# One level of Strassen's algorithm in the gate and up projections of both feed-forward blocks

## The chip, the core and the metric

The kernel runs on one core of a Trainium2 chip. The metric is the device time of one execution in microseconds (us); three runs of the kernel before gave 1392.4, 1393.01 and 1395.76 us, so its median is 1393.01 us. Everything is float32 at the borders.

## The reference, cut to what matters

One encoder layer over 512 tokens of width 1024. It begins and ends with a SwiGLU feed-forward block of inner width 2816; between them stands the token mixing (three kinds of attention, gates, an output projection), which the change leaves alone.

```python
def swiglu(x, w_gate, w_up, w_down):
    return (jax.nn.silu(x @ w_gate) * (x @ w_up)) @ w_down

h = layer_norm(ALPHA * h + 0.5 * swiglu(h, ffn1_w_gate, ffn1_w_up, ffn1_w_down), ln1_g, ln1_b)
mix = token_mixing(h, mem, ...)
h = layer_norm(ALPHA * h + mix, ln2_g, ln2_b)
h = layer_norm(ALPHA * h + 0.5 * swiglu(h, ffn2_w_gate, ffn2_w_up, ffn2_w_down), ln3_g, ln3_b)
```

## The kernel before

Activations lie transposed: xT is 8 tiles (index k) of 128 features by 512 tokens. Every float32 operand of a matmul is held as a pair: hi, the value rounded to float32r by ACT, and lo, the remainder, taken by DVE. A product of two pairs is three matmuls (mm3, L87 to L92): hi by hi, hi by lo, lo by hi, all into one PSUM bank.

Weights come in chunks of 512 KB. wload (L69) gives one load on SP's queue into raw, a ring of 3 buffers; then ACT writes whi (L79) and DVE writes wlo (L80), rings of 4. PE and SP run in the order in which the program is written; ACT, DVE and POOL are ordered by the scheduler, which wload asks to place its work 200 instructions ahead (AHEAD).

A feed-forward block (class FFN, L163) has 22 column tiles f. For each f, mms (L175) runs 8 k for the gate and 8 for the up projection, 48 matmuls of 512 columns, into two banks. act (L180) takes silu of the gate on ACT (L183), multiplies with the up projection on DVE (L184) and splits the result at once into the pair hh, hl, which is kept for all 22 f. down (L195) then multiplies by w_down, once per half of the output width, in 11 chunks c of two f each, with the token tiles t as banks; half of LN (L124) takes the sums out.

The first block starts with hand-written small loads and conversions (xk, wk, L230 to L249). Then come tiles f = 1 to 21 (L256), LN "a" with its pool and the two loads of gain and bias (L113, L114), and two calls of down. The second block runs f = 0 and 1 in two token halves of 256 columns (L901 to L919, while the last token tiles of the normalisation are still on their way), then f = 2 to 21, LN "c", a whole down and then two partial ones: three token tiles, then the last token tile alone with the normalisation of the other three between its chunks.

Pools are a stack on the left side of SBUF and one on the right; a tile that takes the place of a closed pool's tile waits for that tile's last use (`reuse_waits` "tile", L40).

Of the kernel before, what the change touches and what calls it, by code (L numbers as in the profile page):

```python
# [33 lines left out]
def build(tc, a, out):  # L34
# [18 lines left out]
    edge = pool("edge", side="right").tile([P, 24], F32, name="edge")  # L53
    nc.gpsimd.memset(edge, 0.0)
# [14 lines left out]
    def wload(src, n=D, hp=None, lp=None, eng=None, parts=1):  # L69
        with tc.high_priority(offset=AHEAD):  # L70
            raw = wp.tile([P, D], F32, name="raw", tag="raw", bufs=3)
# [91 lines left out]
    class FFN:  # L163
        def __init__(self, n, stack, xT, wgu, wd):
            self.n, self.xT, self.wgu, self.wd = n, xT, wgu, wd
            self.pl = pool("ffn" + n, stack=stack, side="right")
            self.h = {}

        def weight(self, f, j, parts=1):
            return [x.rearrange("p (k c) -> p k c", c=P) for x in wload(self.wgu[f, j], parts=parts)]  # L170

        def weights(self, f):
            return [self.weight(f, j) for j in range(2)]

        def mms(self, w, ps, c):  # L175
            for j in range(2):
                for k in range(KT):
                    mm3(ps[j][:, c], pick(w[j], A, k), pick(self.xT, A, k, c), k == 0, k == KT - 1)

        def act(self, f, ps):  # L180
            sg = self.pl.tile([P, S], F32, name=f"sg{f}", tag="sg", bufs=2)
            hv = self.pl.tile([P, S], F32, name=f"hv{f}", tag="hv", bufs=2)
            nc.scalar.activation(sg, ps[0], AF.Silu)  # L183
            nc.vector.tensor_tensor(out=hv, in0=ps[1], in1=sg, op=OP.mult)  # L184
            h = (self.pl.tile([P, S], F32R, name=f"hh{f}"), self.pl.tile([P, S], F32R, name=f"hl{f}"))
            split(h[0], h[1], hv)
            self.h[f] = h

        def tiles(self, f0, f1):
            for f in range(f0, f1):  # L190
                ps = [bank(f"gu{f}"), bank(f"gv{f}")]
                self.mms(self.weights(f), ps, A)
                self.act(f, ps)

        def down(self, hf, toks, done, order=range(NF // 2), have={}, dest={}, mid=None):  # L195
            ps = {t: bank(f"dn{t}") for t in toks}
            kept = {}
            for n, c in enumerate(order):
                if mid is not None and n in mid:
                    mid[n]()  # L200
                kept[c] = w = have[c] if c in have else [x.rearrange("p (k c) -> p k c", c=S) for x in wload(self.wd[hf, c], **dest.get(c, {}))]
                for j in range(2):
                    f = 2 * c + j
                    for t in toks:
                        mm3(ps[t], pick(self.h[f], A, slice(t * P, (t + 1) * P)), pick(w, A, j),
                            n == 0 and j == 0, n == NF // 2 - 1 and j == 1)
# [9 lines left out]
    s_x = ExitStack()  # L216
    xp = pool("xraw", stack=s_x)

# [4 lines left out]
    xr = xp.tile([P, KT, S], F32, name="xr")  # L223
    wr = [xp.tile([P, D], F32, name=f"wr{j}") for j in range(2)]
    w0 = [[wp.tile([P, D], F32R, name="whi", tag="whi", bufs=4), wp.tile([P, D], F32R, name="wlo", tag="wlo", bufs=4)] for j in range(2)]
    s_ln = ExitStack()
    s_f = ExitStack()
    f1 = FFN("1", s_f, xT, a["wgu1"], a["wd1"])

# [5 lines left out]
    def wk(j, c):  # L235
        nc.sync.dma_start(wr[j][:, c], a["wgu1"][0, j][:, c])
        conv(w0[j][0][:, c], w0[j][1][:, c], wr[j][:, c])

    wk(0, slice(0, 128))
    xk(0, 1)  # L240
    wk(0, slice(128, 512))
    wk(1, slice(0, 512))
    xk(1, 2)
    xk(2, 4)
    wk(0, slice(512, 1024))
    wk(1, slice(512, 1024))
# [3 lines left out]
    s_x.close()  # L250
    ps = [bank("gu0"), bank("gv0")]
    for k in range(KT):
        for j in range(2):
            mm3(ps[j], [x.rearrange("p (k c) -> p k c", c=P)[:, k] for x in w0[j]], pick(xT, A, k), k == 0, k == KT - 1)
    f1.act(0, ps)
    f1.tiles(1, NF)  # L256
# [646 lines left out]
    s_f = ExitStack()  # L903
    f2 = FFN("2", s_f, h2T, a["wgu2"], a["wd2"])
# [11 lines left out]
    for f in range(NS):  # L916
        f2.mms(ws[f], pss[f], slice(256, 512))
        f2.act(f, pss[f])
    s_l2.close()  # L919
    f2.tiles(NS, NF)  # L920
    s_l3 = ExitStack()
    ln3 = LN("c", s_l3, a["ln3_g"], a["ln3_b"], h2_d, spill=out)
# [21 lines left out]
def _pack(inputs):  # L944
# [16 lines left out]
    for i in (1, 2):  # L961
        g, u, d = (f(f"ffn{i}_w_{n}")[0] for n in ("gate", "up", "down"))
        A[f"wgu{i}"] = np.stack([fm(g), fm(u)], 1)
# [68 lines left out]
```

## Time and profile before

| | us |
|---|---|
| median of 3 runs | 1393.01 |
| the profiled execution, its own time | 1392.8 |
| its span, from first to last instruction | 1391.0 |
| PE busy | 1374.2 |
| DVE busy | 656.3 |
| ACT busy | 476.1 |
| POOL busy | 48.8 |

PE is TensorE's matmuls, PEld its weight loads, DVE VectorE, ACT ScalarE, POOL GpSimd, SP the queue of loads. Matmuls overlap, so what one costs in a dense row is the distance from one start to the next, not its duration. In the views of waits the numbers are us in all, times, longest. In the views of stretches an engine's number is its busy time, with its instructions in brackets, then the granted TensorE clock (1.00 is 2.4 GHz, 0.50 is 1.2 GHz), the busy share of the DMA engines and GB/s.

### The profile page before, as it was taken

The numbers are of one execution on the slowest core, as the hardware profiler recorded it, in microseconds if no ns is written. First come the engines' busy times: TensorE is split into PE (matmuls) and PEld (weight loads), VectorE is DVE, ScalarE is ACT, GpSimd is POOL, SyncE is SP. The second block draws the span as 40 slices with busy tenths as digits, with TensorE's granted clock in tenths as the row PEclk, the third lists the DMA queues.
The fourth block names the chain that finished last, engine by engine and source line by source line (L and its number), as shares of the span: only waits on it lengthen the run. The fifth ranks groups of instructions, "written<-read, shape, count | busy, mean of one in ns | idle before, by whom it ended". The sixth has DMA issues, their size and how long they took to land.

```text
span 1391.0 us, 16204 instructions
## 1 busy us (share of the span) xinstructions
PE 1374.2 (99%) x6488; PEld 1152.0 (83%) x6488; DVE 656.3 (47%) x1055; ACT 476.1 (34%) x734; POOL 48.8 (4%) x70
## 2 busy tenths in 40 slices
PE   8999999999999999999999999999999999999997
PEld 6888888888888878988899878888798888888886
DVE  5333333242567995435454655546763333332325
ACT  5222322221245674324334433333342232222210
POOL 0000000000011001001100000000000000000001
PEclk9999999999999999999999999999999999999999
DMA  6323234333346226332223223223743323333241
GB/s 218 101 91 106 92 94 142 112 128 125 113 171 178 59 60 84 106 96 84 80 76 114 77 83 109 74 84 107 256 168 105 105 93 98 100 121 126 90 163 61
DMA packets 49899, 154.80 MB, mean 111 GB/s; under 512 B 9888, under 2 KB 10528, under 8 KB 49824
## 3 DMA queue, kind: packets, MB, share of 16 engines
q1 hardware_dynamic: 44064, 149.51, 32.8%
q0 software_dynamic: 5760, 4.26, 2.3%
q8 instruction: 51, 0.84, 0.2%
q14 instruction: 24, 0.20, 0.0%
HBM read 143.23 MB, written 7.37 MB: 108 GB/s over the span
## 4 chain that ended last, share of the span: by engine, by line
PE 76%; issue 15%; DMA 4%; DVE 3%; ACT 1%; POOL 1%; POOLq 0%; SPq 0%; DVEq 0%; ACTq 0%
PE dn L91 6%; PE dn L92 6%; PE dn L90 6%; PE gu L90 6%; PE gu L91 5%; PE gu L92 5%; PE gv L92 5%; PE gv L90 5%; PE gv L91 5%; DMA x<-dst 2%; PE g L92 2%; PE g L90 2%; PE g L91 2%; PE y L92 1%; PE y L91 1%
## 5 line engine op out<-in xcount | busy, mean ns | idle before, releaser
L79 ACT ACTIVATE whi<-raw 128x1024 fp32r<-128x1024 f32 x237 | 251.3, 1060 | 693.7 <-issue 199.6
L80 DVE TENSOR_TENSOR wlo<-raw,whi 128x1024 fp32r<-128x1024 f32 x237 | 289.6, 1224 | 406.8 <-ACT whi L79 405.8
L90 PE MATMUL dn<-whi,hh 128*128 128x512 f32 x320 | 126.3, 395 | 0.0
L92 PE MATMUL dn<-whi,hl 128*128 128x512 f32 x320 | 126.3, 395 | 0.0
L91 PE MATMUL dn<-wlo,hh 128*128 128x512 f32 x320 | 126.3, 395 | 0.0
L184 DVE TENSOR_TENSOR hv<-gv,sg 128x512 f32<-128x512 f32 x42 | 29.0, 692 | 139.2 <-PE gv L92 138.5
L90 PE MATMUL g<-uh,whi 128*128 128x512 f32 x192 | 75.3, 392 | 0.0
L90 PE MATMUL dp<-uh,whi 128*128 128x512 f32 x192 | 75.1, 391 | 0.0
L92 PE MATMUL g<-uh,wlo 128*128 128x512 f32 x192 | 74.9, 390 | 0.0
L91 PE MATMUL g<-ul,whi 128*128 128x512 f32 x192 | 74.8, 390 | 0.0
L92 PE MATMUL dp<-uh,wlo 128*128 128x512 f32 x192 | 74.7, 389 | 0.0
L91 PE MATMUL dp<-ul,whi 128*128 128x512 f32 x192 | 74.7, 389 | 0.0
L90 PE MATMUL gu<-xh,whi 128*128 128x512 f32 x176 | 69.3, 394 | 4.5 <-ACT xh L220 4.5
L91 PEld LDWEIGHTS dn<-wlo,hh 128*128 128x128 f32 x320 | 60.3, 188 | 14.2
L90 PEld LDWEIGHTS dn<-whi,hh 128*128 128x128 f32 x320 | 60.3, 188 | 14.1
L92 PEld LDWEIGHTS dn<-whi,hl 128*128 128x128 f32 x320 | 60.3, 188 | 14.0
L90 PE MATMUL gv<-xh,whi 128*128 128x512 f32 x176 | 69.1, 393 | 0.3 <-ACT whi L220 0.3
L91 PE MATMUL gu<-xl,whi 128*128 128x512 f32 x176 | 69.3, 394 | 0.0
L92 PE MATMUL gu<-xh,wlo 128*128 128x512 f32 x176 | 69.0, 392 | 0.0
L91 PE MATMUL gv<-xl,whi 128*128 128x512 f32 x176 | 68.9, 392 | 0.0
L92 PE MATMUL gv<-xh,wlo 128*128 128x512 f32 x176 | 68.9, 392 | 0.0
L90 PE MATMUL gu<-h2h,whi 128*128 128x512 f32 x160 | 62.3, 389 | 0.0
(797 smaller groups left out, 2809.0 us busy)
## 6 DMA issues: line engine op xcount, KB each, us to landing
raw<-in_wgu SPq DMA_DIRECT2D x86, 512.0 KB, 3.5
raw<-in_wd SPq DMA_DIRECT2D x47, 512.0 KB, 3.6
raw<-in_wg SPq DMA_DIRECT2D x24, 512.0 KB, 3.7
raw<-in_wdqk SPq DMA_DIRECT2D x24, 512.0 KB, 3.6
raw<-in_wo SPq DMA_DIRECT2D x16, 512.0 KB, 4.3
raw<-in_wv SPq DMA_DIRECT2D x12, 512.0 KB, 3.5
raw<-in_wbr SPq DMA_DIRECT2D x12, 512.0 KB, 3.4
raw<-in_wmk SPq DMA_DIRECT2D x4, 512.0 KB, 3.4
```

The costliest lines, as they stand in the source:

```text
L79: nc.scalar.activation(hi[:, c], raw[:, c], AF.Copy)
L80: (eng or nc.vector).tensor_tensor(out=lo[:, c], in0=raw[:, c], in1=hi[:, c].bitcast(F32), op=OP.subtract)
L90: nc.tensor.matmul(ps, lh, rh, start=first, stop=False, **kw)
L91: nc.tensor.matmul(ps, lh, rl, start=False, stop=False, **kw)
L92: nc.tensor.matmul(ps, ll, rh, start=False, stop=last, **kw)
L184: nc.vector.tensor_tensor(out=hv, in0=ps[1], in1=sg, op=OP.mult)
```

## The change

The input of a block is cut into four quarters (two token halves of 256 by two halves of k), the weights of one f into four blocks (two halves of k by gate and up). For f = 2 to 21 of the first block and f = 3 to 21 of the second, 39 in all, seven products of 12 matmuls of 256 columns (quads) take the place of the 48 matmuls of 512 columns. The sums of the input's quarters are made once per block (sums). The sums of the weights are made for each f (quad_w): three loads on SP, two accumulating DMAs from POOL, two additions on DVE, and then the splits. In the second block the input is first put together again from its pair. The product h is kept in float32 (ha, hb) and split only in down (h_pair). The raw ring moves to a pool of its own on the right; the weights of one f are stored as two chunks, one for each half of k.

```diff
-            h = (self.pl.tile([P, S], F32R, name=f"hh{f}"), self.pl.tile([P, S], F32R, name=f"hl{f}"))
-            split(h[0], h[1], hv)
-            self.h[f] = h
+            nc.vector.tensor_tensor(out=self.h(f), in0=ps[1], in1=sg, op=OP.mult)
...
+        def open(self, stack):
+            n = self.n
+            self.sr = pool("sumr" + n, stack=stack, side="right")
+            self.q = pool("quad" + n, stack=stack)
+            self.X = {i: tuple((self.q if i in (5, 7) else self.sr).tile([P, 4, 256], F32R, name=f"x{i}{z}{n}") for z in "hl") for i in (5, 7, 3, 6)}
+            self.t4 = tuple(self.q.tile([P, 2, S], F32R, name=f"t4{z}{n}") for z in "hl")
+            self.m = {i: self.q.tile([P, 2, 256], F32, name=f"m{i}{n}") for i in (1, 5, 6)}
+
+        def sums(self, xr):
...
+            nc.vector.tensor_tensor(out=t[5], in0=q[1, 1], in1=q[1, 0], op=OP.subtract)
+            split(*self.X[5], t[5])
+            nc.vector.scalar_tensor_tensor(out=t[6], in0=q[0, 0], scalar=-1.0, in1=t[5], op0=OP.mult, op1=OP.subtract)
+            split(*self.X[6], t[6])
+            nc.vector.scalar_tensor_tensor(out=t[3], in0=t[6], scalar=-1.0, in1=q[0, 1], op0=OP.mult, op1=OP.subtract)
+            split(*self.X[3], t[3])
+            nc.vector.tensor_tensor(out=t[7], in0=q[0, 0], in1=q[1, 0], op=OP.subtract)
+            split(*self.X[7], t[7])
...
+        def quad_w(self, f):
+            src = self.wgu[f]
+            with tc.high_priority(offset=AHEAD):
+                r1 = rawp.tile([P, D], F32, name="raw", tag="raw", bufs=3)
+                r3 = rawp.tile([P, D], F32, name="raw", tag="raw", bufs=3)
+                r2 = self.q.tile([P, D], F32, name="raw2", tag="raw2")
+                r4 = self.q.tile([P, S], F32, name="raw4", tag="raw4")
+                nc.sync.dma_start(r1, src[:, :D])
+                nc.sync.dma_start(r2[:, S:], src[:, 3 * S:])
+                nc.sync.dma_start(r3, src[:, S:3 * S])
+                nc.gpsimd.dma_start(r1[:, S:], src[:, :S], accum_op=OP.add)
+                nc.gpsimd.dma_start(r3[:, :S], src[:, 3 * S:], accum_op=OP.add)
+                nc.vector.tensor_tensor(out=r2[:, :S], in0=r1[:, S:], in1=r2[:, S:], op=OP.add)
...
+                split(*w1, r1)
+                w2 = (self.q.tile([P, D], F32R, name="w2h", tag="w2h", bufs=2), self.q.tile([P, D], F32R, name="w2l", tag="w2l", bufs=2))
+                split(*w2, r2)
+                nc.vector.tensor_tensor(out=r4, in0=r2[:, :S], in1=r3[:, S:], op=OP.add)
...
+                split(*w3, r3)
+                w4 = tuple(x[:, f % 2] for x in self.t4)
+                split(*w4, r4)
...
+        def quads(self, f0, f1):
+            def finish(f, W, a, u, sg):
+                self.prod(a, W, 4)
+                nc.scalar.activation(sg[:, 256:], a, AF.Silu)
+                nc.vector.tensor_tensor(out=self.h(f), in0=u, in1=sg, op=OP.mult)
...
+                self.prod(a, W, 1, True)
+                nc.scalar.activation(m[1], a, AF.Copy)
+                self.prod(c, W, 5, True)
+                nc.scalar.activation(m[5], c, AF.Copy)
+                if prev is not None:
+                    finish(*prev)
+                self.prod(a, W, 6)
+                nc.scalar.activation(m[6], a, AF.Copy)
+                self.prod(c, W, 3)
+                nc.vector.scalar_tensor_tensor(out=u[:, :256], in0=c, scalar=-1.0, in1=m[6], op0=OP.mult, op1=OP.subtract)
+                self.prod(d, W, 2)
+                nc.vector.tensor_tensor(out=sg[:, :256], in0=d, in1=m[1], op=OP.add)
+                nc.scalar.activation(sg[:, :256], sg[:, :256], AF.Silu)
+                self.prod(a, W, 7)
+                nc.vector.scalar_tensor_tensor(out=u[:, 256:], in0=a, scalar=-1.0, in1=m[5], op0=OP.mult, op1=OP.subtract)
+                prev = (f, W, a, u, sg)
+            finish(*prev)
...
+        def h_pair(self, c, lo, hi):
+            t = [self.hc.tile([P, 2, S], F32R, name=f"hc{z}", tag=f"hc{z}", bufs=2) for z in "hl"]
+            src = (self.ha if c < 7 else self.hb)[:, 2 * (c % 7):2 * (c % 7) + 2, lo:hi]
+            split(t[0][:, :, lo:hi], t[1][:, :, lo:hi], src)
...
+                with tc.high_priority(offset=AHEAD // 2):
+                    h = self.h_pair(c, toks[0] * P, (toks[-1] + 1) * P)
...
-    f1.tiles(1, NF)
+    f1.sums(xr)
+    f1.tiles(1, 2)
+    f1.quads(2, NF)
+    s_q.close()
+    f1.open_down(s_ln)
...
+    f2.open(s_q)
...
+            nc.vector.tensor_tensor(out=f2.hb[:, k, s_], in0=h2T[0][:, k, s_].bitcast(F32), in1=h2T[1][:, k, s_].bitcast(F32), op=OP.add)
+    f2.sums(f2.hb)
+    f2.tiles(NS, NS + 1)
+    f2.quads(NS + 1, NF)
+    s_q.close()
     s_l3 = ExitStack()
+    f2.open_down(s_l3)
     ln3 = LN("c", s_l3, a["ln3_g"], a["ln3_b"], h2_d, spill=out)
```

## Rows read from the trace of the kernel before

**Rows 1.** The page, busy time of each engine and its share

```profile
PE 1374.2 (99%) x6488; PEld 1152.0 (83%) x6488; DVE 656.3 (47%) x1055; ACT 476.1 (34%) x734; POOL 48.8 (4%) x70
```

**Rows 2.** The view of waits, PE alone

```profile
PE gu L90 <- ACT xh L220: 4.5, 2, 4.4
```

**Rows 3.** The timeline of DVE in the first block: start us, us, instruction

```profile
107.02 0.69 DVE L184 TENSOR_TENSOR hv<-gv,sg 128x512 f32<-128x512 f32 x1 [3.37 <-PE gv L92]
...
117.91 0.69 DVE L184 TENSOR_TENSOR hv<-gv,sg 128x512 f32<-128x512 f32 x1 [3.37 <-PE gv L92]
```

**Rows 4.** The timeline of PE, matmuls of 256 columns, in two places

```profile
370.91 0.28 PE L90 MATMUL mkps<-memh,whi 128*128 128x256 f32 x1
...
374.44 0.28 PE L90 MATMUL mkps<-memh,whi 128*128 128x256 f32 x1
...
1018.93 0.28 PE L90 MATMUL hu<-h2h,whi 128*128 128x256 f32 x1
...
1021.69 0.28 PE L92 MATMUL hu<-h2h,wlo 128*128 128x256 f32 x1
```

**Rows 5.** The page, costliest groups: the two halves of a weight split

```profile
L79 ACT ACTIVATE whi<-raw 128x1024 fp32r<-128x1024 f32 x237 | 251.3, 1060 | 693.7 <-issue 199.6
L80 DVE TENSOR_TENSOR wlo<-raw,whi 128x1024 fp32r<-128x1024 f32 x237 | 289.6, 1224 | 406.8 <-ACT whi L79 405.8
```

**Rows 6.** Instructions by tile, duration ns (least/median/most): 256 columns out of PSUM

```profile
L284 ACT ACTIVATE mk<-mkps x4: 363/364/364, 374.8 to 383.3; 128x256 f32<-128x256 f32 x4
...
L628 DVE TENSOR_TENSOR dp<-ds,bias x16: 410/415/421, 636.3 to 796.6; 128x256 f32<-128x256 f32 x16
```

**Rows 7.** The view of DMA issues: queue, count, KB each, median us to landing

```profile
raw<-in_wgu SPq DMA_DIRECT2D x86, 512.0 KB, 3.5
...
k<-kr POOLq DMA_DIRECT2D x8, 128.0 KB, 2.4
...
bias<-in_dbias POOLq DMA_DIRECT2D x4, 256.0 KB, 5.3
...
uel<-ul POOLq DMA_DIRECT2D x2, 256.0 KB, 6.7
...
cb<-in_ln_b SPq DMA_DIRECT2D x1, 512.0 KB, 6.2
```

**Rows 8.** The timeline of SP's queue, end of the gate and up part

```profile
212.86 0.43 SPq L67 DMA_DIRECT2D ag<-in_ln_g  x1
...
217.93 22.09 SPq L76 DMA_DIRECT2D raw<-in_wd  x5
...
1207.87 16.64 SPq L76 DMA_DIRECT2D raw<-in_wgu  x4
...
1225.04 0.42 SPq L67 DMA_DIRECT2D cb<-in_ln_b  x1
```

**Rows 9.** The timeline of PE, its first matmuls and its last

```profile
4.37 0.80 PE L90 MATMUL gu<-xh,whi 128*128 128x512 f32 x1 [4.37 <-ACT xh L220]
...
11.06 0.61 PE L92 MATMUL gv<-xh,wlo 128*128 128x512 f32 x1
11.48 0.42 PE L90 MATMUL gu<-xh,whi 128*128 128x512 f32 x1
...
1382.38 0.40 PE L92 MATMUL dn<-whi,hl 128*128 128x512 f32 x1
```

**Rows 10.** Busy time in stretches: PE, PEld, DVE, ACT, POOL, clock, DMA

```profile
0.00:30.00 30.00, 25.14 (x94) 19.00 (x95) 15.30 (x18) 16.31 (x20) 0.37 (x6) 1.00 0.73 243
...
1015.00:1043.00 28.00, 27.09 (x218) 26.31 (x217) 18.01 (x26) 9.71 (x13) 2.77 (x2) 1.00 0.39 137
...
1375.00:1380.00 5.00, 5.00 (x23) 4.07 (x22) 4.67 (x7) 0.00 (x0) 2.16 (x2) 1.00 0.27 111
...
1385.00:1387.00 2.00, 0.00 (x0) 0.00 (x0) 1.56 (x3) 0.00 (x0) 1.26 (x1) 1.00 0.00 0
1387.00:1389.00 2.00, 0.00 (x0) 0.00 (x0) 0.71 (x2) 0.00 (x0) 0.00 (x0) 0.52 0.55 206
```

More of the change, by code (lines that the diff above doesn't have):

```diff
@@ L53, in build @@
     edge = pool("edge", side="right").tile([P, 24], F32, name="edge")
+    rawp = pool("rawp", side="right")
     nc.gpsimd.memset(edge, 0.0)
@@ L70, in wload @@
         with tc.high_priority(offset=AHEAD):
-            raw = wp.tile([P, D], F32, name="raw", tag="raw", bufs=3)
+            raw = rawp.tile([P, D], F32, name="raw", tag="raw", bufs=3)
             hi = wp.tile([P, D], F32R, name="whi", tag="whi", bufs=4) if hp is None else hp
@@ L166, in __init__, with h @@
             self.pl = pool("ffn" + n, stack=stack, side="right")
-            self.h = {}
-        def weight(self, f, j, parts=1):
-            return [x.rearrange("p (k c) -> p k c", c=P) for x in wload(self.wgu[f, j], parts=parts)]
+            self.ha = self.pl.tile([P, 14, S], F32, name=f"ha{n}")
+            self.hb = self.pl.tile([P, 8, S], F32, name=f"hb{n}")
+        def h(self, f):
+            return self.ha[:, f] if f < 14 else self.hb[:, f - 14]
         def weights(self, f):
-            return [self.weight(f, j) for j in range(2)]
+            return [[x.rearrange("p (j k c) -> p j k c", j=2, c=P) for x in wload(self.wgu[f][:, i * D:(i + 1) * D])] for i in range(2)]
         def mms(self, w, ps, c):
@@ new lines, in prod @@
+        def prod(self, ps, W, i, first=False):
+            for k in range(4):
+                mm3(ps, pick(W[i], A, k), pick(self.X[i], A, k), first and k == 0, k == 3, skip_group_check=True)
+        def quads(self, f0, f1):
[3 more added lines that the diff above has]
+                nc.vector.tensor_tensor(out=self.h(f), in0=u, in1=sg, op=OP.mult)
+            prev = None
+            for f in range(f0, f1):
+                W = self.quad_w(f)
+                b1, b2 = bank(f"ga{f}"), bank(f"gc{f}")
+                a, d, c = b1[:, :256], b1[:, 256:], b2[:, :256]
+                m = {i: x[:, f % 2] for i, x in self.m.items()}
+                u = self.q.tile([P, S], F32, name=f"u{f}", tag="u", bufs=2)
+                sg = self.q.tile([P, S], F32, name=f"sg{f}", tag="sg", bufs=2)
+                self.prod(a, W, 1, True)
[15 more added lines that the diff above has]
+            finish(*prev)
@@ L221, in conv @@
         nc.vector.tensor_tensor(out=lo, in0=raw, in1=hi.bitcast(F32), op=OP.subtract)
-    xr = xp.tile([P, KT, S], F32, name="xr")
-    wr = [xp.tile([P, D], F32, name=f"wr{j}") for j in range(2)]
-    w0 = [[wp.tile([P, D], F32R, name="whi", tag="whi", bufs=4), wp.tile([P, D], F32R, name="wlo", tag="wlo", bufs=4)] for j in range(2)]
     s_ln = ExitStack()
     s_f = ExitStack()
+    s_q = ExitStack()
     f1 = FFN("1", s_f, xT, a["wgu1"], a["wd1"])
+    f1.open(s_q)
+    xr = f1.hb
+    wr = [rawp.tile([P, D], F32, name="raw", tag="raw", bufs=3) for j in range(2)]
+    w0 = [[wp.tile([P, D], F32R, name="whi", tag="whi", bufs=4), wp.tile([P, D], F32R, name="wlo", tag="wlo", bufs=4)] for j in range(2)]
     def xk(k0, k1):
@@ L917, in build @@
         f2.mms(ws[f], pss[f], slice(256, 512))
+    s_l2.close()
+    f2.open(s_q)
+    for f in range(NS):
         f2.act(f, pss[f])
-    s_l2.close()
-    f2.tiles(NS, NF)
+    for j in range(2):
+        for c in range(2):
+            k, s_ = slice(4 * j, 4 * j + 4), slice(256 * c, 256 * c + 256)
+            nc.vector.tensor_tensor(out=f2.hb[:, k, s_], in0=h2T[0][:, k, s_].bitcast(F32), in1=h2T[1][:, k, s_].bitcast(F32), op=OP.add)
[3 more added lines that the diff above has]
+    s_q.close()
     s_l3 = ExitStack()
+    f2.open_down(s_l3)
     ln3 = LN("c", s_l3, a["ln3_g"], a["ln3_b"], h2_d, spill=out)
@@ L962, in _pack @@
         g, u, d = (f(f"ffn{i}_w_{n}")[0] for n in ("gate", "up", "down"))
[L963 removed]
+        A[f"wgu{i}"] = np.ascontiguousarray(np.stack([fm(z).reshape(NF, P, 2, S) for z in (g, u)], 3)).reshape(NF, P, 2 * D)
         A[f"wd{i}"] = np.stack([tm(np.ascontiguousarray(d[:, :S])), tm(np.ascontiguousarray(d[:, S:]))])
```

47 lines of the change are left out of this document (29 added, 18 removed).

## The prediction

> **What bounds the kernel now.** I read the page's busy times first, then the waits, then the timelines of the two feed-forward blocks, and last the queues. PE is busy 99% of the span, DVE 47%, ACT 34% [rows 1], and the longest wait that PE has for anyone is 4.5 us in all, at the very start [rows 2]. So PE's row is dense, and what counts is how many matmuls stand in it and how far apart. In the first block one f takes 117.91 - 107.02 = 10.89 us [rows 3]: 48 matmuls of 512 columns, 0.227 us from start to start. Everything else (weight loads, splits, the multiplication) lies beside that.
>
> The sum is made against the profiled execution, 1392.8 us (its span of 1391.0 and 1.8 around it); the median of the runs, 1393.01, is 0.2 above it. About 0.3%, 4.2 us, is what a measurement of this kernel can tell from no change: 1388.8 to 1397.2.
>
> **Products for products.** An f gets 7 x 12 = 84 matmuls of 256 columns. Such matmuls are in the trace. In the key projection of the memory 30 of them take 374.44 - 370.91 = 3.53 us, 0.118 each; at the head of the second block 23 take 1021.69 - 1018.93 = 2.76 us, 0.120 each [rows 4]. Half of the columns thus cost 52 to 53%, not 50%. The operands X1, X2 and X4 are slices of xT as in the second place, the other four are small tiles as in the first, so I take 0.119: 84 x 0.119 = 10.0 us, a gain of 0.89 per f and of 39 x 0.89 = 34.7 us, **-35**. Bounds: 0.120 gives -32, 0.118 gives -38.
>
> The Trainium skill, page "TensorE: Matmul & The Clock Gate", section "Back-to-back issue gap", puts the distance at columns / 2.4 + 2.5 ns, 109 at 256 columns and 216 at 512. Worked out from it (an estimate) the sum would have 39 x (48 x 0.216 - 84 x 0.109) = -46 here. The trace disagrees at both widths, and the measured distances stand.
>
> **The other engines, per f.** DVE loses one split of 512 columns and two of 1024, and gets three of 1024 (1.22 each [rows 5]), one of 512, two additions and the last multiplication (about 0.69 each, as hv [rows 3]) and three operations of 256 columns out of PSUM (0.41 each [rows 6]): 7.7 us of 10.0, somewhat less where neighbours overlap. ACT gets three halves of a split (1.06 [rows 5]), one of 512 columns and five operations of 256 (0.36 [rows 6]): 5.6 us. Both fit under PE, but DVE's slack falls from some 7 us per f to 2.5, and it works in order: behind an addition that waits for a DMA stand the operations that empty PSUM, and PE waits for those. SP's queue carries 1.25 MB per f instead of 1, POOL's 0.5 MB more.
>
> **The accumulating DMA** is not in the trace. A weight sum now takes a load, then (POOL waits for its landing) an accumulating DMA, then the split, before its raw buffer is free, with 3 buffers for two such tiles per f, and one for r2. The tightest loop that I find goes from the load of r2 of one f to that of the third f after it: issue 0.4, r3's load 4.0, accumulate A, split 1.06 + 1.22, r1's load 4.0, accumulate A, addition 0.69, split 1.06 + 1.22, addition 0.69. That is 14.3 + 2A, and some 1 us of waiting in line at DVE; a load of 512 KB lands in 3.5 us [rows 7], and 4.0 allows for the denser queue. It stays under three f of PE (30 us) while A is below 7.3 us. Bounds for A from the rows: 2.4 us (128 KB between tiles, POOL's queue) below, 6.7 for 256 KB in small pieces [rows 7]; above, twice a plain POOL load of 256 KB, 10.6, if reading the target costs as much as the source. The nearest row is the plain load, 5.3 [rows 7]; with the read of the target and the other traffic I take 6.5. So PE still sets the pace in the likeliest case, at 0, and the loop is the first rival.
>
> The Trainium skill, page "DMA: Bandwidth & Descriptors", section "Anatomy of one DMA — SWDGE (gpsimd) path", fits such a DMA with 2.0 us + bytes / 436 GB/s: 2.6 us for 256 KB. By it (an estimate) the loop would be 20.5 us and would never bind; the trace has 5.3 for the same bytes, so the rival keeps its chance.
>
> **From up to down.** SP issues in program order: gain and bias of the normalisation go out at 212.86, ahead of the first chunk of w_down, which goes out from 217.93 on [rows 8], long before its matmul. In the new kernel the LN pool stands where the quad pool stood, after 16 KB of hc: by the order in which tiles are made its gain and bias fall on t4, which the very last product of the block reads. So SP waits for PE's last product, and the loads of w_down stand behind it in the queue. Then PE is idle for: gain, bias and chunk, three loads of 512 KB in a row. In the trace such a row (the last of the four wgu loads, whose issue ends at 1207.87 + 16.64 = 1224.51, then cg and cb) lands at 1225.04 + 6.2 = 1231.2 [rows 7, 8], 6.7 us after that and some 7.0 after its start. Then 1.06 on ACT [rows 5], and DVE's 1.22 less one matmul: 9 us. TensorE's clock then has to be won back: after its last matmul at 1382.38 the stretch from 1385 is still granted 1.00 (2.4 GHz), that from 1387 on 0.52 [rows 9, 10], so a pause of 9 us ends at 1.2 GHz. In the start of the kernel matmuls stand 0.42 us apart until 11.48, 7.1 us after the first [rows 9]; half of that, 3.5, is lost again. Sum 12 us per block, **+24**. Bounds: 0 if the tiles lie otherwise; the chunk alone 0.9 + 3.5 + 1.06 = 5.5 per block, 11; at most 12.5, 25. I take the upper end because nothing else stands in PE's or SP's order at that place.
>
> **The entries.** sums adds four additions and four splits of 1024 columns, 8 x 1.22 = 9.8 us of DVE, per block. In the first 30 us DVE is busy 15.3 [rows 10]; with 9.8 and the first weight set (5) it is full when the first product wants X5. In the second block four more additions (4.9) come first: with sums and a weight set 20 us of new work, against 10 us free in the stretch from 1015 to 1043 [rows 10] and some 7 in the one full tile that follows (10.9 less 3.8 of DVE). I take 2 and 3, **+5**; bounds 0 and 15 (all of sums late once).
>
> **Down.** The splits that act drops come back in h_pair, for each half and once more for the last token tile. Beside chunks of four or three token tiles (24 or 18 matmuls, 4 to 5.6 us) they are hidden: 2.4 of DVE and 2.1 of ACT each. In the last stretch a chunk is 6 matmuls, 1.4 us, and DVE is busy 4.67 of 5 us [rows 10]; 11 splits of 256 columns at 0.4 add 4.4, of which I put **+3** on the path (0 to 4.4). The new order of the stored weights and of the first loads moves the same bytes and is free; the ring's new place too.
>
> Sum: 1392.8 - 34.7 + 24 + 5 + 3 = **1390**. This case by itself ranges from 1382 to 1400.
>
> **Rivals.** (1) The raw ring sets the pace: slower. It decides from A = 7.3 us on; with A = 8 an f takes 31.3 / 3 = 10.4, +17, 1407; with A = 10 11.8, +69, 1459. For it: POOL's loads are already the slowest per byte [rows 7], a load and an accumulate in series for every buffer, DVE nearly full. Against: the plain load of that size is 2 us below the point. (2) SP is not held, because the tiles fall on memory that is free early: the wd loads go out in time, 24 us less, 1366. For it: I know the placing from the program only. Against: most of that pool is in use until the last product. (3) Columns alone set the distance of dense products, 0.1135 at 256: -53 instead of -35, 1372. Against it stand both places of [rows 4]. The Trainium skill's formula, above, has this shape.
>
> **Chances.** Forecast 0.37 (of that 0.11 below 1388.8, 0.16 within, 0.10 above), ring 0.35 (0.02 faster, 0.03 within, 0.30 slower), SP not held 0.20 (0.19 faster, 0.01 within), columns alone 0.05 (faster), anything else 0.03 (slower). Faster 0.37, within 0.20, slower 0.43. The range reaches down into rival 2 and up to A of about 8.7, 1364 to 1428.
>
> **What would show it.** Right: products 0.118 to 0.120 us apart and an f in about 10.0 us; in both blocks a pause of PE of about 9 us before the first dn matmul, with SP's gain load waiting for PE, and a clock of 0.50 after it. Wrong: waits of PE for wlo or for DVE in every f and POOL's accumulating DMAs landing after 7.3 us or more (rival 1); gain and bias issued before the last product (rival 2); products 0.114 apart (rival 3). A pause of 5 us at one of the entries would make my +5 wrong.

## The result, and the profile after

The changed kernel takes 1511.65 us (median of four runs, 1506.31 to 1515.59) against 1392.96 for the kernel before, measured beside it: a ratio of 1.0845, interval 1.0807 to 1.0884. The forecast was 1390.0 with a range up to 1428. The profiled execution took 1509.97, its span is 1508.1.

The page of the changed kernel, busy times and the granted clock in 40 slices:

```profile
PE 1384.2 (92%) x7892; PEld 1220.3 (81%) x7892; DVE 857.5 (57%) x1359; ACT 613.3 (41%) x987; POOL 115.1 (8%) x148
...
PEclk9999999899999999999999999999999999998999
```

PE has 10 us more of busy time than before [rows 1] although it does less work, and 124 us in which it does nothing. Where they are, the view of waits tells (PE alone):

```profile
PE ga L91 <- DVE sg L274: 61.8, 39, 2.1
PE dn L91 <- ACT whi L80: 18.1, 2, 9.8
PE gc L91 <- ACT m L266: 11.2, 15, 2.0
PE ga L91 <- ACT m L264: 6.3, 2, 4.5
```

Before, the only one of note was 4.5 us at the start [rows 2]. Now product 7, which adds to the accumulator a, waits in all 39 f, 1.6 us on the mean, until DVE has made sg out of d, the accumulator of product 2. It does not need sg; but a and d are the two halves of one PSUM bank, b1 in the program. The two waits for whi are the pauses from up to down.

By stages, from the timelines of PE (first instruction to first dn matmul, from there to the first hg matmul of the second block, to its first dn matmul, to the end of the span), in us, with two of the experiments told below. A pause ahead of a first dn matmul is part of the up column:

| | up, block 1 | down and middle | up, block 2 | down and end |
|---|---|---|---|---|
| before | 248.2 | 767.9 | 243.8 | 131.1 |
| after | 299.1 | 772.3 | 300.5 | 136.3 |
| own bank, later gain and bias (e4) | 245.0 | 770.3 | 239.0 | 135.4 |
| and no accumulating DMAs (e7) | 235.2 | 774.6 | 232.9 | 134.3 |

Of the 117 us between the spans, 108 lie in the two gate and up parts. One turn of an f there, from the timeline of the changed kernel (SP, POOL, DVE and PE; the number in brackets is the idle time before, and who ended it):

```profile
94.99 0.33 SPq L224 DMA_DIRECT2D raw<-in_wgu  x1
...
100.36 0.87 POOL L227 DMA_DIRECT2D raw<-in_wgu  x1 [5.00 <-DMA raw<-in_wgu]
...
105.93 0.69 DVE L229 TENSOR_TENSOR raw<-raw,raw 128x512 f32<-128x512 f32 x1 [4.03 <-DMA raw<-in_wgu]
106.54 2.35 DVE L86 TENSOR_TENSOR wlo<-raw,whi 128x1024 fp32r<-128x1024 f32 x2
...
107.79 0.33 SPq L224 DMA_DIRECT2D raw<-in_wgu  x1
...
110.95 1.21 DVE L86 TENSOR_TENSOR w2l<-raw,w2h 128x1024 fp32r<-128x1024 f32 x1
112.09 0.41 DVE L274 TENSOR_TENSOR sg<-ga,m 128x256 f32<-128x256 f32 x1
112.55 0.39 PE L91 MATMUL ga<-x7h,whi 128*128 128x256 f32 x1 [2.11 <-DVE sg L274]
...
114.31 0.41 PE L91 MATMUL ga<-xh,whi 128*128 128x256 f32 x1
114.52 0.41 PE L92 MATMUL ga<-xl,whi 128*128 128x256 f32 x1
```

Read it as a ring. r1 is loaded (94.99), POOL's accumulating DMA goes out when that has landed (100.36) and has landed by 105.93, DVE adds (L229), and only behind this addition in DVE's queue stand two splits. The first is that of r3 of the f before; when it ends, at 107.7, its raw buffer is free and SP issues the next r1: 12.8 us after the last one. L229 starts at 93.13, 105.93, 117.72 and 129.61; over 14 turns of the first block (81.50 to 257.25) it is 12.55 us per f, where the forecast had 10.0. Down the same queue sg stands behind the addition, six more operations and w2l, and PE waits for it. After this pause the matmuls stand 0.21 us apart for 3 us instead of 0.12. The view of stretches (columns as in [rows 10]) has the clock for it, and for two longer stretches of the steady part:

```profile
112.50:117.30 4.80, 4.75 (x27) 4.75 (x28) 0.42 (x1) 1.67 (x3) 0.27 (x1) 0.64 0.74 192
117.30:124.00 6.70, 6.70 (x58) 6.70 (x58) 5.32 (x8) 3.88 (x7) 0.86 (x1) 1.00 0.56 128
...
120.00:180.00 60.00, 51.15 (x391) 49.73 (x390) 33.51 (x48) 25.04 (x42) 8.54 (x10) 0.94 0.60 142
180.00:240.00 60.00, 52.69 (x419) 51.47 (x418) 35.10 (x50) 26.99 (x46) 8.64 (x10) 0.97 0.61 153
```

The end of the gate and up part, from the same kernel's timeline (SP, PE), and the clock after the pause:

```profile
290.79 0.33 SPq L68 DMA_DIRECT2D ag<-in_ln_g  x1
...
291.68 10.22 SPq L77 DMA_DIRECT2D raw<-in_wd  x5
...
299.08 0.80 PE L91 MATMUL dn<-whi,hch 128*128 128x512 f32 x1 [8.21 <-ACT whi L80]
...
299.08:303.00 3.92, 3.45 (x7) 2.44 (x8) 3.66 (x3) 2.11 (x2) 0.00 (x0) 0.50 0.51 165
```

Gain, bias and chunk go out only when PE has made its last product, as forecast; before, they went out at 212.86 and 217.93, 30 us ahead of their use [rows 8].

The view of DMA issues, which answers [rows 7]:

```profile
raw<-in_wgu SPq DMA_DIRECT2D x86, 512.0 KB, 4.9
raw<-in_wgu POOLq DMA_DIRECT2D x78, 256.0 KB, 5.4
```

The accumulating DMA takes 5.4 us from issue to landing, the load 4.9 instead of 3.5.

### The profile page after: what moved, and what is told of

The parts are those of the page before. It is cut to its first block, busy times and chain, and to the rows that moved or that the text cites. A ratio compares the mean times of both kernels' runs of the same rounds, so it can differ in the third digit from the quotient of the medians.

```text
span 1508.1 us, 20211 instructions
## 1 busy us (share of the span) xinstructions
PE 1384.2 (92%) x7892; PEld 1220.3 (81%) x7892; DVE 857.5 (57%) x1359; ACT 613.3 (41%) x987; POOL 115.1 (8%) x148
## 4 chain that ended last, share of the span: by engine, by line
PE 45%; DMA 23%; issue 19%; DVE 10%; ACT 2%; POOL 1%; SPq 0%; DVEq 0%; POOLq 0%; ACTq 0%
DMA raw<-in_wgu 16%; PE dn L92 5%; PE dn L93 5%; PE dn L91 5%; PE ga L91 2%; PE g L93 2%; PE g L91 2%; PE g L92 2%; DMA x<-dst 2%; PE ga L93 2%; PE ga L92 2%; DVE wlo L86 2%; DVE w2l L86 2%; DMA raw<-in_wd 2%; PE y L93 1%
## 5 line engine op out<-in xcount | busy, mean ns | idle before, releaser
L91 PE MATMUL dn<-whi,hch 128*128 128x512 f32 x320 | 128.4, 401 | 18.1 <-ACT whi L80 18.1
L92 PE MATMUL dn<-wlo,hch 128*128 128x512 f32 x320 | 128.3, 401 | 0.9 <-DVE wlo L81 0.9
L93 PE MATMUL dn<-whi,hcl 128*128 128x512 f32 x320 | 127.9, 400 | 0.1
L91 PE MATMUL ga<-x7h,whi 128*128 128x256 f32 x156 | 51.9, 333 | 61.8 <-DVE sg L274 61.8
L229 DVE TENSOR_TENSOR raw<-raw,raw 128x512 f32<-128x512 f32 x39 | 27.0, 693 | 128.3 <-DMA raw<-in_wgu 128.3
L91 PEld LDWEIGHTS ga<-x7h,whi 128*128 128x128 f32 x156 | 32.7, 210 | 69.8 <-DVE sg L274 69.8
L91 PEld LDWEIGHTS dn<-whi,hch 128*128 128x128 f32 x320 | 61.5, 192 | 32.7 <-ACT whi L80 18.5
L92 PEld LDWEIGHTS dn<-wlo,hch 128*128 128x128 f32 x320 | 61.3, 192 | 16.1 <-DVE wlo L81 1.9
L93 PEld LDWEIGHTS dn<-whi,hcl 128*128 128x128 f32 x320 | 61.4, 192 | 14.7 <-DVE hcl L86 0.5
L86 DVE TENSOR_TENSOR hcl<-ha,hch 128x1024 fp32r<-128x1024 f32 (+2 forms) x35 | 35.1, 1009 | 50.8 <-ACT hch L85 50.8
L85 ACT ACTIVATE hch<-ha 128x1024 fp32r<-128x1024 f32 (+2 forms) x35 | 30.8, 885 | 72.4 <-PE dn L92 69.4
```

The costliest lines, as they stand in the source:

```text
L85: nc.scalar.activation(hi, src, AF.Copy)
L86: nc.vector.tensor_tensor(out=lo, in0=src, in1=hi.bitcast(F32), op=OP.subtract)
L91: nc.tensor.matmul(ps, lh, rh, start=first, stop=False, **kw)
L92: nc.tensor.matmul(ps, lh, rl, start=False, stop=False, **kw)
L93: nc.tensor.matmul(ps, ll, rh, start=False, stop=last, **kw)
L229: nc.vector.tensor_tensor(out=r2[:, :S], in0=r1[:, S:], in1=r2[:, S:], op=OP.add)
```

## The experiments

Two theories stood at first: BANK (PE is held by DVE's read of the other half of its bank) and SUPPLY (the weight sets come late). With e10 a sharper form of the second came up: LOOP, the ring above. Ratios are against the kernel before, run beside each; its medians there were 1396.1 to 1396.8 us, against 1392.96 beside the changed kernel, so versions are compared by their ratios. A point is one hundredth of the time before, 14 us.

**e1: d in a bank of its own.**

```diff
-                b1, b2 = bank(f"ga{f}"), bank(f"gc{f}")
-                a, d, c = b1[:, :256], b1[:, 256:], b2[:, :256]
+                b1, b2, b3 = bank(f"ga{f}"), bank(f"gc{f}"), bank(f"gd{f}")
+                a, d, c = b1[:, :256], b3[:, :256], b2[:, :256]
...
-                self.prod(d, W, 2)
+                self.prod(d, W, 2, True)
```

> The second product's sum d gets a PSUM bank of its own; before it shared one with a. Theory BANK (the seventh product waits for DVE to have read d, because both lie in one bank, 61.8 us in all): those waits go, and with them most of the pauses after which the clock is granted at half; 1508 falls to 1425 to 1450. Theory SUPPLY (load, accumulating DMA and splits set the pace of an f): PE waits for something else instead, mostly for a weight split, and the time falls by less than 15 us, to 1495 or more.

Measured: 1414.95 us, ratio 1.0133 (1.0079 to 1.0186), 97 us less than the changed kernel and 10 below BANK's range. The waits for sg are gone from the view of waits; PE's longest are now

```profile
PE dn L91 <- ACT whi L80: 18.8, 2, 9.8
PE gc L91 <- ACT m L266: 7.0, 6, 2.2
```

This looked like BANK alone. But it gained 35 us more than the waits for sg, and the timeline (DVE, SP) shows that the scheduler, too, had made something else of it: the split of r3 stands ahead of the addition.

```profile
101.25 1.23 DVE L86 TENSOR_TENSOR wlo<-raw,whi 128x1024 fp32r<-128x1024 f32 x1 [0.79 <-ACT whi L85]
102.50 0.33 SPq L224 DMA_DIRECT2D raw<-in_wgu  x1
104.65 0.69 DVE L229 TENSOR_TENSOR raw<-raw,raw 128x512 f32<-128x512 f32 x1 [2.18 <-DMA raw<-in_wgu]
```

SP's next load of r1 goes out at 102.50, before the addition: the ring is open. One edit had changed two things.

**e2: no accumulating DMAs** (the two lines of `nc.gpsimd.dma_start(..., accum_op=OP.add)` are left out; the bank is shared).

> Leaves out both accumulating DMAs of every f, so two of the seven weight sums lack an addend. SUPPLY: an f is no longer paced by them and falls from about 13.0 to 10.0 to 10.5 us, 1508 to about 1400 to 1415. BANK: the seventh product still waits for DVE's read of d, which stands behind splits; only what those splits waited for the DMA is saved; 1460 to 1490.

Measured: 1450.45, ratio 1.0387 (1.0340 to 1.0434), between the two; PE still waits for sg 45.9 us (39 times, up to 1.6), and an f takes 11.5 us. Neither theory explains all of it by itself.

**e3: gain and bias later,** with the first residual tiles in the middle of the first half of down, so that they stand in SP's queue behind five chunks of w_down and no longer hold these up. (Some expectations below call this edit "gain and bias early"; the loads that come early by it are those of w_down.)

```diff
-            load(self.g, g.rearrange("(o d) -> o d", o=1).broadcast_to([P, D]))
-            load(self.b, b.rearrange("(o d) -> o d", o=1).broadcast_to([P, D]))
+            self.gb = [(self.g, g), (self.b, b)]
...
         def pre(self, hf, toks):
+            for t, v in self.gb:
+                load(t, v.rearrange("(o d) -> o d", o=1).broadcast_to([P, D]))
+            self.gb = []
```

> Gain and bias of each normalisation are loaded together with its first residual tiles instead of ahead of the first chunk of the down weights. Theory HOLD (SP waits with these two loads for the last product, and the down weights stand behind them): the two pauses of 8 to 10 us ahead of the first dn matmul shrink to under 3 us, and the time falls by 18 to 25 us, to 1483 to 1490. Rival: the first chunk is late in any case, because its raw buffers or splits are; the pauses stay and the time falls by less than 5 us.

Measured: 1494.43, ratio 1.0702 (1.0653 to 1.0751), 17 us less as it stands, above the forecast's 1490, and 1.4 points or 20 us less by the ratios. The pauses of 8.2 and 9.8 fall to 1.4 each, for h's split:

```profile
PE dn L91 <- ACT hch L85: 2.8, 2, 1.4
```

**e4: e1 and e3 together.**

> Both edits, the bank of its own and the later loads of gain and bias. If BANK and HOLD hold and are independent, the savings add: 1405 to 1430, still above the kernel before (1391). If SUPPLY holds, 1475 to 1485.

Measured: 1391.88 (eight runs), ratio 0.9975 (0.9949 to 1.0001), about the time before. This is below the range for savings that add, which had been made before e1 was known; e1's 7.1 and e3's 1.4 points make 8.5, and e4 has 8.7. In the steady part PE is dense, as the timeline and the stretches of e4 show:

```profile
99.53 0.28 PE L91 MATMUL ga<-x7h,whi 128*128 128x256 f32 x1
...
109.53 0.28 PE L91 MATMUL ga<-x7h,whi 128*128 128x256 f32 x1
```

```profile
120.00:180.00 60.00, 60.00 (x505) 59.89 (x504) 42.19 (x60) 32.53 (x54) 9.93 (x12) 1.00 0.72 183
```

An f takes 10.0 us, 84 matmuls 0.119 us apart, at full clock: the forecast's own number.

**e5: d in the other half of c's bank** (`d = b2[:, 256:]`).

> The second product's sum d goes to the other half of c's bank instead of a's. BANK, read generally (PE may not write into a bank while DVE has still to read from it, whichever half): the waits move from the seventh product to the second, which now waits for DVE's read of c; that read stands ahead of a split in DVE's order, not behind one, so 0.6 to 1.5 us per f, 25 to 60 us in all, and 1435 to 1490. Rival: it is only the seventh product that suffers, by its place in the order; then the time is that of the bank of its own, about 1415.

Measured: 1452.86, ratio 1.0408 (1.0350 to 1.0466), as BANK has it. DVE has the split ahead of the addition here, as in e1, so this is the price of a shared bank with the ring open. PE now waits for u, the reader of c, before product 2 may go into the other half:

```profile
PE gc L91 <- DVE u L272: 28.5, 39, 4.8
```

That the wait moves with d shows that sharing makes it. But the profile takes who ended a wait from semaphores, which the program sets; in every run the halves of one bank were also halves of one tile of the program. Whether the program guards by tile or by bank, and what the chip would do without the guard, no run shows.

**e6: the six operations that empty PSUM at a higher priority** in the scheduler, bank shared.

> The bank stays shared as in the changed kernel; the operations of ACT and DVE that empty PSUM (copies m, both u, the sum of d) are put ahead of the weight work in the scheduler's order. If the wait is made of two things, the shared bank and DVE's order (the read of d stood behind an addition and a split), the seventh product's waits fall from 1.6 to about 0.7 us per f, 61.8 to 25 to 35 in all, fewer pauses at half clock, and 1435 to 1475. If DVE's order has no part in it, 1495 or more; if it is all, 1420 or less.

Measured: 1514.55, ratio 1.0850 (1.0818 to 1.0881). The scheduler left DVE's order as it was (sg still right behind w2l), so the run tells nothing of either theory, nor of what another order would do.

**e10: product 2 earlier,** so that a whole product into another bank stands between d and the next product into a's bank.

```diff
+                self.prod(d, W, 2)
+                nc.vector.tensor_tensor(out=sg[:, :256], in0=d, in1=m[1], op=OP.add)
+                nc.scalar.activation(sg[:, :256], sg[:, :256], AF.Silu)
                 if prev is not None:
                     finish(*prev)
...
-                self.prod(d, W, 2)
-                nc.vector.tensor_tensor(out=sg[:, :256], in0=d, in1=m[1], op=OP.add)
-                nc.scalar.activation(sg[:, :256], sg[:, :256], AF.Silu)
```

> The bank stays shared and gain and bias stay late, but product 2 is made before the previous f's product 4, so that one whole product (1.43 us at full clock) into other banks stands between d's last matmul and product 6, the next one into its bank. BANK (PE's product waits until DVE has read the other half; nothing but the missing distance makes the loss): PE was kept for 2.1 us at the worst and 1.6 on the mean with nothing in between, so per f only 0 to 0.7 us are left, the waits for sg fall from 62 us to under 15, f to 10.1 to 10.6 us, and the time to 1412 to 1440, as with a bank of its own (1415). Rival ROW (it is not the bank, but DVE's order, which comes late with whatever is behind it): the products behind d wait as long as before, at another place, 1490 to 1515.

Measured: 1457.61, ratio 1.0434 (1.0420 to 1.0448): missed by both. PE still waits 42.1 us for sg. The timeline of e10 (DVE, PE) says why, and gave the idea of LOOP:

```profile
161.51 0.69 DVE L229 TENSOR_TENSOR raw<-raw,raw 128x512 f32<-128x512 f32 x1 [2.01 <-DMA raw<-in_wgu]
162.12 1.22 DVE L86 TENSOR_TENSOR wlo<-raw,whi 128x1024 fp32r<-128x1024 f32 x1
163.25 0.42 DVE L268 TENSOR_TENSOR sg<-ga,m 128x256 f32<-128x256 f32 x1
...
163.72 0.38 PE L91 MATMUL ga<-x6h,w2h 128*128 128x256 f32 x1 [0.81 <-DVE sg L268]
```

DVE stands 2 us at an addition that waits for a transfer; d is ready by the time that it lands, but sg has its place behind the addition and a split. The same with e3's edit and the first quad of each block one f later, e11:

> The shared bank with the new order of products, gain and bias early, first quads one f later. If distance in PE's row does as much as a bank of its own: within 8 us of the run with the bank, 1378 to 1394. If each f still waits some 0.3 us for d's reader and loses clock by it: 1395 to 1415.

1433.3, ratio 1.0266 (1.0252 to 1.0281): the shared bank still costs, as in the second of the two forecasts, and more.

**e12: r3 out of the raw ring,** bank shared, DVE's order unchanged.

```diff
-                r3 = rawp.tile([P, D], F32, name="raw", tag="raw", bufs=3)
+                r3 = self.q.tile([P, D], F32, name="raw3", tag="raw3", bufs=2)
```

> The changed kernel with r3 in two buffers of its own instead of in the raw ring; a and d still share a bank and DVE's order is the same. LOOP (the raw ring sets the pace: load 4.9, accumulate 5.4, addition and split 1.9, issues 0.7, 12 to 13 us per f): that loop is open now, and what is left per f is the chain from product 3 over ACT's split of w2 and DVE's to sg, as in the run without accumulating DMAs (f 11.5, waits of 1.2 for sg): f 11.3 to 11.7, 1440 to 1465, waits for sg of 40 to 50 us. BANK alone (the wait for DVE's read is all there is): nothing changes, 1495 to 1515, f about 13, waits for sg about 62 us.

**e13: a bank for d, and a second buffer for r2,** with which the scheduler put the addition ahead of r3's split again.

```diff
-                r2 = self.q.tile([P, D], F32, name="raw2", tag="raw2")
+                r2 = self.q.tile([P, D], F32, name="raw2", tag="raw2", bufs=2)
```

> d in a bank of its own as in the run at 1415, and a second buffer for r2, which for itself only lets a load go out earlier. With it the scheduler puts DVE's addition ahead of the split of the previous f's r3 again, as in the changed kernel. LOOP: though nobody waits for a bank any more, the ring of three sets the pace again at 11.8 to 13 us per f, PE waits for weight splits or for ACT and DVE instead of for sg, 1465 to 1515. BANK alone: as with the bank, 1405 to 1420, f 10.0 to 10.4.

Measured: e12 1461.3, ratio 1.0469 (1.0447 to 1.0491); e13 1449.63, ratio 1.0379 (1.0363 to 1.0396). e12 came as LOOP has it: an f takes 11.5 us and PE waits 45.8 us for sg. e13 lies between the two ranges: the ring does set its pace, but goes round in 10.95 us on the mean (14 turns of L229 from 77.15 to 230.46), because load and accumulate take only 4.2 and 4.1 us in the turn below. PE waits there for u (29.9 us in all), which stands behind the addition. Timeline of e13 (SP, POOL, DVE; the accumulate's line names u as what ended its wait, on the next turn, at 161.21, it names the load):

```profile
146.03 0.33 SPq L224 DMA_DIRECT2D raw<-in_wgu  x1
...
150.26 0.86 POOL L227 DMA_DIRECT2D raw<-in_wgu  x1 [7.69 <-DVE u L272]
...
154.34 0.69 DVE L229 TENSOR_TENSOR raw<-raw,raw 128x512 f32<-128x512 f32 x1 [2.24 <-DMA raw<-in_wgu]
...
155.29 2.35 DVE L86 TENSOR_TENSOR wlo<-raw,whi 128x1024 fp32r<-128x1024 f32 x2
...
156.53 0.33 SPq L224 DMA_DIRECT2D raw<-in_wgu  x1
```

What the shared bank leaves with the ring open is a chain that e12's timeline shows (ACT, DVE, PE):

```profile
151.48 1.06 ACT L85 ACTIVATE w2h<-raw 128x1024 fp32r<-128x1024 f32 x1 [0.93 <-PE gc L92]
152.57 1.23 DVE L86 TENSOR_TENSOR w2l<-raw,w2h 128x1024 fp32r<-128x1024 f32 x1 [0.53 <-ACT w2h L85]
153.71 0.42 DVE L274 TENSOR_TENSOR sg<-ga,m 128x256 f32<-128x256 f32 x1
154.19 0.39 PE L91 MATMUL ga<-x7h,whi 128*128 128x256 f32 x1 [1.24 <-DVE sg L274]
```

When product 3 has read w2h for the last time, ACT fills that buffer for a later f, DVE splits the rest, and only then takes sg; all that has the 1.43 us of product 2 (12 x 0.119) to hide in.

The four runs make a square of ratios:

| | ring closed by DVE's order | ring open |
|---|---|---|
| a and d in one bank | 1.0845 (after) | 1.0469 (e12) |
| d in its own | 1.0379 (e13) | 1.0133 (e1) |

The bank costs 4.7 or 3.4 points (65 or 47 us of 1396), the ring 3.8 or 2.5 (52 or 34). Each is real without the other, and together they cost 7.1 points or 99 us, 1.3 points or 18 us more than the two alone. Of these four runs only the changed kernel has a clock below 1 in the steady part (0.94 and 0.97 from 120 to 240 us, 1.00 in the others, as this stretch of e12 has it).

```profile
120.00:180.00 60.00, 53.80 (x443) 52.78 (x442) 36.78 (x51) 28.90 (x47) 8.64 (x10) 1.00 0.65 165
```

An estimate from span and mean granted clock of the four (what the clock lacks to 1, times the span: 40.7, 21.9, 26.0 and 22.6 us for the changed kernel, e12, e13 and e1) gives 15 us of those 18; that the clock accounts for them is argued, not shown. Nor is the square pure: e12 has two raw buffers more in all, e13 one.

**The entries.** e4's span is 1.4 us shorter than that of the kernel before, though 39 f at 10.0 should give 35 less. Eight runs looked for the rest, all with e4's two edits.

e7, e4 with e2's two lines left out:

> Bank of its own and later gain and bias, and besides without the two accumulating DMAs per f (two of the seven weight sums lack an addend). SUPPLY (the three raw buffers with load and accumulate in series set the pace once the bank is out of the way): an f falls below 10.0 us or waits inside the f vanish, under 1378. NO SUPPLY: an f is 10.0 us as before, and only the first f of each block, where sets are still being made, gain something; 1380 to 1390 against 1392.

Measured: 1376.08, ratio 0.9858 (0.9813 to 0.9903), by time in SUPPLY's range. But nothing changes in the steady part (505 and 506 matmuls in 60 us), so supply does not set the pace there; the gain lies in the two gate and up stages (table above: 9.8 and 6.1 us). That the stage between is 4.3 longer is scatter: where its code is the same, it takes 770.3 to 776.4 us. In e4 the view of waits has 12 us for ACT's copies m at the two entries, in e7 none of note. The edit takes away the transfers' bytes as well as their place behind the loads, so it does not tell the two apart.

e8 (e6's priorities on e4):

> Bank of its own, later gain and bias, and the emptying operations first. What is left of waits (PE for ACT's copies m at the entry of both blocks, 12.9 us in all, and the clock after them) stood behind weight splits in ACT's order: theory ENTRY says they fall to under 5 us and the time to 1375 to 1386. Rival: the entries wait for the sums themselves, the copies are only where it shows; no more than 3 us.

1398.66, ratio 1.0009 (0.9987 to 1.0032): no gain. e9 (`f1.tiles(1, 3)`, `f1.quads(3, NF)`, and one f later in the second block):

> A bank for d, gain and bias early, and the first quad of each block one f later (37 quads instead of 39), so that the sums of the input and the first weight sums have one more f of 10.9 us to be ready. ENTRY (the loss against the forecast's +5 lies in the first two or three quads, which wait for ACT's copies behind the sums' and sets' splits): the waits for m fall from 12 us to under 4 and the clock there stays at 0.97 and more, 8 to 16 us less than 1391.9 and 1.8 more for two quads fewer: 1378 to 1386, 0.987 to 0.993 of before. Rival LOAD (the waits come from the first weight sets, which come late whenever they begin): 1390 to 1396.

1398.13, ratio 1.0007 (0.9997 to 1.0018): the waits come later and are as long. e14 (e12's edit on e4):

> The bank for d and gain and bias early (1391.9), and r3 out of the raw ring. In the steady part nothing changes (f 10.0, PE dense). At the entries the loads of the first two sets no longer wait for a buffer of the ring: if the entry's waits (12 us and the clock after them) come from the ring there, 4 to 12 us less, 1380 to 1388; if they come from load and accumulate in series, which stay, 1389 to 1395.

1395.29, ratio 0.9994 (0.9984 to 1.0004): no gain, so it is not the buffers. Then the sums without a second transfer, e15, since both addends already lie in SBUF:

```diff
-                nc.gpsimd.dma_start(r1[:, S:], src[:, :S], accum_op=OP.add)
-                nc.gpsimd.dma_start(r3[:, :S], src[:, 3 * S:], accum_op=OP.add)
+                nc.gpsimd.tensor_tensor(out=r1[:, S:], in0=r1[:, :S], in1=r1[:, S:], op=OP.add)
+                nc.gpsimd.tensor_tensor(out=r3[:, :S], in0=r2[:, S:], in1=r3[:, :S], op=OP.add)
```

> Bank for d, gain and bias early, and POOL adds the two halves in SBUF (both lie there already: src's first quarter in r1, its last in r2) instead of two accumulating DMAs. SERIES (the entry waits because load and accumulate, 5 us each, stand one behind the other): the entries come near those of the run without sums, 1376.1, if one addition of 128x512 takes POOL not much longer than DVE's 0.69: 1374 to 1384, 0.985 to 0.991 of before. If POOL needs 3 us or more for it, or holds DVE up, the gain is lost and f rises above 10.0: 1390 to 1410. If the two transfers in series were not the cause: 1388 to 1395.

1413.51, ratio 1.0115 (1.0094 to 1.0136): above the worst of the three forecasts, the one in which POOL holds DVE up. With e12's edit on top, e16:

> The same with r3 out of the raw ring. With sums made in SBUF the ring has slack, so no difference to e15 beyond 3 us: 1374 to 1384; a rival by which the ring still holds the first loads up gives 4 to 8 us less than e15.

1416.93, ratio 1.0145 (1.0130 to 1.0160): no better. The groups of instructions in e15, line, engine, shapes and count, then busy us and mean ns:

```profile
L230 POOL TENSOR_TENSOR raw<-raw,raw 128x512 f32<-128x512 f32 x39 | 66.5, 1704 | 259.6 <-DMA raw<-in_wgu 244.8 <-DVE wlo L86 14.8
...
L86 DVE TENSOR_TENSOR t4l<-raw,t4h 128x512 fp32r<-128x512 f32 x39 | 56.5, 1449 | 0.0
```

and the same DVE group in e4:

```profile
L86 DVE TENSOR_TENSOR t4l<-raw,t4h 128x512 fp32r<-128x512 f32 x39 | 26.7, 685 | 0.0
```

POOL takes 1.7 us, and DVE's operation beside it twice its time. Last, DVE itself for the first two f of a block (e17), or three (e18):

```diff
+                if sbuf:
+                    nc.vector.tensor_tensor(out=r1[:, S:], in0=r1[:, :S], in1=r1[:, S:], op=OP.add)
+                    nc.vector.tensor_tensor(out=r3[:, :S], in0=r2[:, S:], in1=r3[:, :S], op=OP.add)
+                else:
...
+                W = self.quad_w(f, f < f0 + 2)
```

> Bank for d, gain and bias early; for the first two f of each block DVE adds the halves in SBUF (0.69 us each, 2.8 per block) instead of two accumulating DMAs per f; all others as before. SERIES (at the entry a set is late because its accumulating DMA starts when the load has landed and takes 7 to 8 us there): the first two sets are ready 5 us and more earlier and the waits for m fall from 12 us to under 5: 1376 to 1384, 0.986 to 0.992. Rival DVE (DVE is full at the entries, so its extra 5.5 us stand on the path): 1390 to 1397.

> The same for the first three f of each block. SERIES: within 4 us of the run with two. Rival DVE: 1 to 3 us more than that.

e17 1392.27, ratio 0.9974 (0.9953 to 0.9994); e18 1394.85, 0.9995 (0.9979 to 1.0012): the rival DVE. The sets are there earlier, but DVE is now busy almost without a gap from 21.8 to 38 us, and PE waits for the input's sums. The timeline of PE and the stretch are those of an execution of e17 that took 1399.67, 7 us over its median; the second stretch is that of e7:

```profile
36.87 0.39 PE L92 MATMUL ga<-x6l,w2h 128*128 128x256 f32 x1 [2.72 <-DVE x6l L86]
41.42 0.58 PE L91 MATMUL gc<-x3h,w2h 128*128 128x256 f32 x1 [2.79 <-ACT x3h L85]
...
21.80:38.00 16.20, 13.29 (x74) 11.37 (x73) 15.88 (x18) 8.37 (x11) 1.03 (x1) 1.00 0.48 134
...
21.80:38.00 16.20, 14.95 (x88) 13.11 (x87) 15.78 (x18) 10.50 (x15) 0.00 (x0) 1.00 0.56 191
```

DVE is as full in e7, where PE never waits more than 1.3 us for such a sum, so a full DVE is not by itself the cause: what it does first counts too. At the entries either the weight sets or the input's sums are late. Which order of DVE's work there would serve both stays open. No version that makes all sums (e7 does not) beats the kernel before by the 0.3% that the prediction took for what a measurement can tell: e17, the best with e4, is 0.26% below it.

## Why the prediction was wrong

The result is 122 us above the forecast. Bank and ring together have 99 of them (the square); the rest lies at the entries and in down. Two steps of the prediction failed, and both are terms that it had put at 0.

**Products for products: right.** The products stand 0.119 us apart and an f takes 10.0, in e4, where nothing stands in PE's way. Rival 3 (0.114) falls.

**The other engines, per f: this step failed.** It counted DVE's 7.7 of 10.0 us and said that behind an addition that waits for a DMA stand the operations that empty PSUM, and that PE waits for those; then it gave that wait no price and took "both fit under PE" as the end of it. Busy time told nothing here: DVE is 57% busy and still every f is late. Two things were missing. First, that a and d are one bank, so that product 7 must wait for a read of d that it does not need, 61.8 us in all; nothing but DVE's place in line decides how long. The Trainium skill, page "PSUM — Partial Sum Buffer", section "PSUM bank collisions raise a hardware error", asks to guard PSUM with semaphores by bank (more finely by bank and group of 32 partitions) and not by address, since two engines in one bank at once are an error there even at different columns. The trace agrees as far as it goes: with d in the bank of a (61.8 us of waits) or of c (28.5, e5), PE is held; with a bank of its own, not. The forecast should have asked of each product which engine reads the rest of its bank at that time. Second, the ring.

**The accumulating DMA: this step failed too, not by the size but by the loop.** A was 5.4 us, inside the bounds; 6.5 was taken. The Trainium skill's fit of 2.6, from the page "DMA: Bandwidth & Descriptors", section "Anatomy of one DMA — SWDGE (gpsimd) path", is half of what the trace has. The loop of 14.3 + 2A for three f supposed that DVE splits one f's r3 before the next f's addition. DVE's queue has them the other way round, and that closes a loop with one f per turn: on the turn shown 5.4 us from load to accumulate, 5.6 to its landing, 0.6 for the addition, 1.2 for the split, 12.8 against PE's 10.0. With these other three terms A would have to stay under 2.8. Rival 1 was therefore right in kind (the ring sets the pace), and wrong in its point of 7.3 and its price; of the signs given for it, PE's waits for DVE in every f came, a landing after 7.3 us did not. By the square the bank has 47 to 65 and the ring 34 to 52 of the 122 us between forecast and result.

**From up to down: right.** SP's gain load waits for PE's last product, the pauses are 8.2 and 9.8 us for the 9 forecast, the clock behind the first is 0.50, and taking the cause away gave 20 us (e3) and 1.6 points, 22 us, in e4, of the 24. Rival 2 falls.

**The entries: wrong by 19 us.** Per block -15.8 and -13.9 were forecast without the pause (20 and 19 f at 0.89, less 2 and 3). e4 has 245.0 - 248.2 = -3.2 and 239.0 - 243.8 = -4.8, and 1.4 of each is the wait for h's first split, which stands ahead of the first dn matmul: -4.6 and -6.2 without it. Without accumulating DMAs (e7) it is in the same way -14.4 and -12.3, close to the forecast: DVE's share was counted, the accumulating DMA behind the load, before a first set is ready, was not. e17, where DVE took that work over for the first two sets, gained nothing, so DVE's order counts there too, and the cause is not fully settled. That e4, without the pauses, still comes near the forecast of 1390 is luck: it has none of the 24 us forecast for them and loses about as much elsewhere, most of it at the entries.

**Down: about right.** +3 was forecast for the last stretch; e4's last stage has 4.3 more than before (2.6 to 6.3 over all versions). The 2.4 more of the stage before it lie within its scatter.

## What to carry to other kernels

A busy share says that an engine has time, not that it has it when it is asked: follow, in the order of its queue, what stands ahead of each operation that empties PSUM, and what that one waits for. Where a bank is free, give every accumulator that is emptied on its own a bank of its own. And where a buffer ring is refilled by transfers, work out the loop with the order in which the scheduler queued the releases, not the order of the program; one edit can turn that order, so look at it again in every experiment before giving the edit the credit.

## What was not expected of the hardware

- POOL adding two 128x512 tiles in SBUF takes 1.7 us, and a DVE operation of two SBUF inputs beside it goes from 0.69 to 1.45 us on the mean (e15). The Trainium skill, "GPSIMD Engine Reference", section "Key points", says that the two share their SBUF interfaces and contend where DVE has two SBUF inputs; the trace agrees, and u, which takes one of its inputs from PSUM, stays at 0.41 us in e15.
- A pause of PE of 2.1 us in an else dense row was followed by 3 us at half clock (matmuls 0.21 us apart, 0.64 granted over the stretch), which costs about 1.4 us more. In the first block of the changed kernel, from 60 us on, eight pauses are 2.0 to 2.1 us long; five were followed so, three were not. e12's pauses of 1.24 us left the clock at 1.00.
- The accumulating DMA (256 KB) lands after 5.4 us, as a plain POOL load of that size does in 5.3 [rows 7], and after 4.4 in e13: a price for reading the target cannot be seen.
